# A two-block transformer kernel on one core: tokens stationary in 1024-column gemms, seven-product tiles, and low halves made by an adding DMA

## The chip, the cores and the metric

The kernel runs on one core of a Trainium2 chip. The metric is device time in microseconds, as the median of the runs; lower is better. Engines are called by their names: TensorE (PE in the profile, its weight loads PEld), VectorE (DVE), ScalarE (ACT), GpSimd (POOL) and SyncE (SP), which issues the loads.

## What is computed

Two transformer blocks over one sequence of 256 tokens, model width 2048, all in fp32. Shortened from the reference:

```python
def first_block(x, ...):
    h = rmsnorm(x, norm_attn[l])
    proj = h @ w_in[l]                       # 2048 x 6144
    ...                                      # 8 dilated heads (ya), 8 differential heads (yb)
    x = x + jnp.concatenate([ya, yb], axis=-1) @ w_out[l]
    h = rmsnorm(x, norm_ffn[l])
    x = x + (jax.nn.silu(h @ w_gate[l]) * (h @ w_up[l])) @ w_down[l]      # inner width 5632
    return rmsnorm(x, norm_final)

def second_block(x, ...):
    z = jnp.einsum('bsd,de->bse', rmsnorm_2(x, norm1_g[l]), w_in[l])
    ...                                      # 8 forgetting-attention heads, 4 mLSTM heads
    merged = (g_a * jnp.einsum('bse,ed->bsd', a_out, w_proj_a[l])
              + g_m * jnp.einsum('bse,ed->bsd', m_out, w_proj_m[l]))
    x = x + jnp.einsum('bsd,de->bse', merged, w_out[l])
    h2 = rmsnorm_2(x, norm2_g[l])
    u = causal_dwconv(jnp.einsum('bsd,df->bsf', h2, w_up[l]), conv_w[l], conv_b[l])
    ...
    return x + jnp.einsum('bsf,fd->bsd', jax.nn.silu(u_gate) * u_val, w_down[l])
```

In the text w_out, w_gate, w_up and w_down are the first block's; those of the second have a _2.

## The kernel before

Every weight is read once from HBM, and nearly all work is matrix products with them. A product of fp32 precision is made of three products of float32r operands: a number is cut into a high half (the cast to float32r) and a low half (the rest), and hi·hi, hi·lo and lo·hi are summed in PSUM. The activations are cut once and kept; the weights are cut as they arrive. `raw_tile` (L66) loads up to 2048 columns of 128 partitions into one of three buffers through SP's queue. `split` (L72) makes the halves of 1024 columns: ScalarE casts `wh` (L76), VectorE subtracts it from the raw weight and writes `wl` (L77). The pool `sp` has four slots for `wh` and four for `wl`, so these two engines run at most four halves ahead of TensorE.

There are two forms of product. In `xstat` (L102; the three attention inputs of the first block, and most of the second's) the tokens are the stationary operand and 512 weight columns move: six products of 512 columns for 128 rows of the weight and 512 of its columns, three for each half of the 256 tokens (L119 to L121). In `wstat` (L92) with `mm_w` (L80) a 128x128 block of the weight is stationary, and the tokens move: `wh` meets the 512 columns that hold the tokens' high and low halves side by side (L81), `wl` the 256 high ones (L82). Its result has features on the partitions and tokens along the row, as the residual `resid` has, so that the next stage takes it without a transpose:

```python
    def mm_w(ps, wh, wl, x, start, stop):
        pe.matmul(ps, wh, x, start=start, stop=False)
        pe.matmul(ps[:, 1, :], wl, x[:, 0, :], start=False, stop=stop)
```

`wstat` carries w_out (with a loop of its own, L384 to L404), w_gate, w_up, w_down, the mLSTM's q and k, the gates of the second block, its two projections, w_out_2, w_up_2 and w_down_2. Each result of 128 features is added to the residual as soon as it is done (L398, L399, L421, L422, L770, L771), and `hilo` cuts the new piece at once for the next stage. `Acc` (L176) gathers its squares for the norm, with an add on POOL (L188). The factor of the norm, one per token, lies along the row, and VectorE multiplies each result by it (`evac`, L408). The two feed-forward stages run in four parts of 11 chunks of the inner width: gate and up for these, then w_down over these into the residual.

PSUM is two pools of four banks, `psd` for the weight products and `psa` for all else. The order of the instructions on each engine is set when the program is built, by a scheduler that runs its own timeline; on the chip each engine keeps to it.

Of the kernel before, what the change touches and what calls it, by code (L numbers as in the profile page):

```python
# [23 lines left out]
QC = 11  # L24
NQ = FC // QC
# [5 lines left out]
GA_EARLY = 6  # L31
WARM = 8

# [19 lines left out]
def body(ctx: ExitStack, tc: tile.TileContext, xT, gp, cst, rst, w1, wo1, wg, wu, wd,  # L53
         wgate, wmo, wmv, wmq, wmk, wfox, wga, wgm, wpr, wo2, wup, wd2, out):
# [4 lines left out]
    xp = ctx.enter_context(tc.tile_pool(name="xp", bufs=16))  # L59
# [3 lines left out]
    psd = ctx.enter_context(tc.tile_pool(name="psd", bufs=4, space=PSUM))  # L63
    psa = ctx.enter_context(tc.tile_pool(name="psa", bufs=4, space=PSUM))
# [7 lines left out]
    def split(raw, a, b):  # L72
        wh = sp.tile([P, 1024], F32R, tag="wh", name="wh")
        wl = sp.tile([P, 1024], F32R, tag="wl", name="wl")
        n = b - a
        act.copy(wh[:, :n], raw[:, a:b])  # L76
        dve.tensor_sub(wl[:, :n], raw[:, a:b], wh[:, :n].bitcast(F32))  # L77
        return wh, wl

    def mm_w(ps, wh, wl, x, start, stop):  # L80
        pe.matmul(ps, wh, x, start=start, stop=False)  # L81
        pe.matmul(ps[:, 1, :], wl, x[:, 0, :], start=False, stop=stop)  # L82

    def dps():
        t = psd.tile([P, 2, S], F32, tag="d", name="d")
        return t

    def aps():
        t = psa.tile([P, 512], F32, tag="a", name="a")
        return t  # L90

    def wstat(ps, src, xs, first=True, last=True):  # L92
        raw = raw_tile(src)
        n = len(xs)
        h = (n + 1) // 2
        for a, b in ((0, h), (h, n)):
            wh, wl = split(raw, a * P, b * P)
            for k in range(a, b):
                o = (k - a) * P
                mm_w(ps, wh[:, o:o + P], wl[:, o:o + P], xs[k],  # L100
                     first and k == 0, last and k == n - 1)

    def xstat(src4, xr, pre=(), then=None):
        p0 = psd.tile([P, 512], F32, tag="d", name="d")
        p1 = psd.tile([P, 512], F32, tag="d", name="d")
        pp = (p0, p1)
        for q in range(4):
# [3 lines left out]
            for h, kn in ((0, 1), (1, 1), (2, 2)) if pre and q == 0 else ((0, 2), (2, 2)):  # L111
                wh, wl = split(raw, h * 512, (h + kn) * 512)
                for kk in range(kn):
                    k = q * 4 + h + kk
                    a, b = wh[:, kk * 512:(kk + 1) * 512], wl[:, kk * 512:(kk + 1) * 512]
                    for t in range(2):
                        xh = xr[k][:, 0, t * P:(t + 1) * P]
                        xl = xr[k][:, 1, t * P:(t + 1) * P]
                        pe.matmul(pp[t], xh, a, start=k == 0, stop=False)  # L119
                        pe.matmul(pp[t], xh, b, start=False, stop=False)  # L120
                        pe.matmul(pp[t], xl, a, start=False, stop=k == KC - 1)  # L121
        return pp

    def chunk(tag):
        t = xp.tile([P, 2, S], F32R, tag=tag, name=tag)
        return t

    def hilo(dst, src, scale=None):
        if scale is None:
            act.copy(dst[:, 0, :], src)  # L130
            dve.tensor_sub(dst[:, 1, :], src, dst[:, 0, :].bitcast(F32))
        else:
            act.activation(dst[:, 0, :], src, AF.Copy, scale=scale)
            dve.scalar_tensor_tensor(dst[:, 1, :], src, scale, dst[:, 0, :].bitcast(F32),  # L134
                                     op0=ALU.mult, op1=ALU.subtract)
# [5 lines left out]
    resid = xin[:, 16:].rearrange("p (k s) -> p k s", k=KC)  # L141
# [17 lines left out]
    def sumsq(acc):  # L159
        ps = aps()  # L160
        for t in range(2):
            pe.matmul(ps[:, t:t + 1], acc[:, t * P:(t + 1) * P], ones[:, 0:1], start=True, stop=True)
        return ps

    def bcast(r, name):
# [3 lines left out]
        ps = aps()  # L169
# [5 lines left out]
    class Acc:  # L175
        def __init__(self, name):  # L176
            self.acc = np_.tile([P, S], F32, tag=name, name=name)
            self.first = True

        def add(self, src, scale=None):  # L180
            kw = {} if scale is None else {"scale": scale}
            if self.first:
                act.activation(self.acc, src, AF.Square, **kw)
                self.first = False
            else:
                sq = np_.tile([P, S], F32, tag="sq", name="sq", bufs=2)
                act.activation(sq, src, AF.Square, **kw)  # L187
                pool.tensor_add(self.acc, self.acc, sq)  # L188

    warm = cp.tile([P, 1], F32, name="warm")  # L190
    act.copy(warm, ones[:, 0:1])
    pw = aps()
# [3 lines left out]
    first = []  # L196
    raw0 = rp.tile([P, 2048], F32, tag="raw", name="raw")
    for a, b in ((0, 1), (1, 2), (2, 4), (4, 8), (8, 12), (12, 16)):
# [4 lines left out]
        for k in range(a, b):  # L203
            c = chunk("x")
            hilo(c, resid[:, k, :], gx[:, k:k + 1])
            xr.append(c)
# [5 lines left out]
    y1 = []  # L212
    with tc.tile_pool(name="a1", bufs=1) as ap1:
# [5 lines left out]
        pool.tensor_mul(sqx, resid[:, 0:4], resid[:, 0:4])  # L219
        for i in range(1, 4):  # L220
            sqi = ap1.tile([P, 2, 4, S], F32, tag="qk", name="sqi", bufs=3)[:, 0]
            pool.tensor_mul(sqi, resid[:, 4 * i:4 * i + 4], resid[:, 4 * i:4 * i + 4])
# [4 lines left out]
        def consts():  # L227
            for d, src in ((cst_t, cst), (rst_t, rst), (gp_t, gp)):
# [22 lines left out]
        def rope_T(pp, name, hb, r2, co, so):  # L251
# [13 lines left out]
            for j in range(2):  # L265
                ps = aps()
# [24 lines left out]
        def attn_a(qT, kT, v, h):  # L291
            ps = aps()
# [16 lines left out]
            c = chunk("y")  # L309
            hilo(c, po[:, :S])  # L310
            y1.append(c)

        def attn_b(qT, kT, v, h, on, ss):
            smc, dnc = [], []
            for c in range(2):
                ps = aps()
# [27 lines left out]
            for qt in range(2):  # L344
                sq = np_.tile([P, S], F32, tag="sq", name="sq", bufs=2)
                act.activation(sq[:, :P], pv[:, qt], AF.Square, accum_out=ss[:, qt, h:h + 1])

        for grp in range(4):
# [18 lines left out]
            else:  # L367
# [7 lines left out]
                for h in range(4):  # L375
                    for t in range(2):
                        dve.tensor_scalar_mul(on[:, t, h, :], on[:, t, h, :], ss[:, t, h:h + 1])
                    ps = aps()
                    for t in range(2):
                        pe.transpose(ps[:, t * P:(t + 1) * P], on[:, t, h, :], ident)  # L380
                    c = chunk("y")
                    hilo(c, ps[:, :S], g08[:, 0:1])
                    y1.append(c)

        acc = Acc("acc")
        xr = []
        for half in range(2):
            for n2 in range(8):
                raw = raw_tile(wo1[half * 8 + n2])
                for j in range(2):  # L390
                    n = n2 * 2 + j
                    wh, wl = split(raw, j * 1024, (j + 1) * 1024)
                    ps = dps()
                    for k in range(8):
                        o = k * P
                        mm_w(ps, wh[:, o:o + P], wl[:, o:o + P], y1[8 * half + k], k == 0, k == 7)
                    t = ap1.tile([P, 2, S], F32, tag="sm", name="res", bufs=3)[:, 0]
                    dve.tensor_add(t, ps[:, 1], resid[:, n])  # L398
                    dve.tensor_add(resid[:, n], ps[:, 0], t)  # L399
                    if half == 1:  # L400
                        c = chunk("x")
                        hilo(c, resid[:, n], gain(G_FFN, n))
                        xr.append(c)
                        acc.add(resid[:, n])  # L404
        r = rtok_from(sumsq(acc.acc)[:, 0:2], "rtok", EPS)
        rb = bcast(r, "rb")

    def evac(fp, ps, rb, tag, bufs=2):  # L408
        t = fp.tile([P, S], F32, tag="ev", name="ev", bufs=3)
        act.copy(t, ps[:, 1])  # L410
        dve.tensor_add(t, ps[:, 0], t)  # L411
# [494 lines left out]
```

## Time and profile before

| | |
|---|---|
| time, median of three runs | 2571.62 us (2570.88 to 2572.28) |
| span of the profiled execution, first to last instruction | 2569.7 us |
| TensorE busy, products | 2553.7 us, 99%, 14040 |
| TensorE busy, weight loads (beside the products) | 2199.0 us, 86%, 14040 |
| VectorE busy | 1753.5 us, 68%, 2726 |
| ScalarE busy | 1317.2 us, 51%, 2069 |
| POOL busy | 72.3 us, 3%, 73 |
| read from HBM | 465.35 MB, 182 GB/s over the span |

The profiled execution has no time of its own beside its span; the runs of the table are other executions of the same program. The profile counts the time in which an engine had an instruction in work. TensorE's products overlap (one starts before the one ahead has ended), so their durations add up to more than the time they take; the pitch, from one start to the next, is what a product costs in a stream. VectorE's and ScalarE's instructions overlap a little too. A product's operands are written `d<-x,wh`: output, then moving and stationary operand in either order.

### The profile page before, as it was taken

How to read it: one execution, taken by the hardware profiler on the slowest of the kernel's cores; microseconds unless marked ns; L12 is line 12 of the kernel's file. 1: busy time of each engine (PE TensorE's matmuls, PEld its weight loads, DVE VectorE, ACT ScalarE, POOL GpSimd, SP SyncE). 2: the span in 40 equal slices, each digit the busy share in tenths (PEclk: the TensorE clock that was granted, in tenths of full speed). 3: DMA queues.
4: the chain of work that ended last, by engine and by line, in shares of the span. 5: the costliest groups of instructions: out<-in, count | busy, mean ns of one | idle time of the engine just before them, and what ended most of it. 6: DMA issues, size and time to landing. Idle time of an engine off the chain costs nothing.

```text
span 2569.7 us, 35839 instructions
## 1 busy us (share of the span) xinstructions
PE 2553.7 (99%) x14040; PEld 2199.0 (86%) x14040; DVE 1753.5 (68%) x2726; ACT 1317.2 (51%) x2069; POOL 72.3 (3%) x73
## 2 busy tenths in 40 slices
PE   8999999999999999999999999999999999999999
PEld 6888888888888888888888888888888888888888
DVE  7666578666666666677465566667777776776776
ACT  4555446444444444465455655545554554554553
POOL 3000001000000000031000000001000000000000
PEclk9999999999999999999999999999999999999999
DMA  6444445545545545545544455555555555645555
GB/s 246 152 158 170 168 164 186 191 168 209 182 172 203 186 166 205 184 165 197 186 159 164 165 182 187 197 188 182 193 184 173 208 186 171 212 171 190 198 175 168
DMA packets 73466, 469.78 MB, mean 183 GB/s; under 512 B 8144, under 2 KB 10448, under 8 KB 28496
## 3 DMA queue, kind: packets, MB, share of 16 engines
q1 hardware_dynamic: 70992, 465.38, 51.5%
q8 instruction: 110, 1.80, 0.3%
q10 hardware_dynamic: 2304, 2.10, 0.2%
q14 instruction: 60, 0.49, 0.1%
HBM read 465.35 MB, written 2.10 MB: 182 GB/s over the span
## 4 chain that ended last, share of the span: by engine, by line
PE 99%; DVE 0%; DMA 0%; issue 0%; SPq 0%; ACT 0%
PE d L81 51%; PE d L82 26%; PE d L120 6%; PE d L121 6%; PE d L119 6%; PE a L279 1%; PE a L286 0%; PE a L340 0%; PE a L270 0%; PE a L308 0%; DMA raw<-in_w 0%; DVE x L134 0%; PE d L481 0%; PE a L662 0%; PE a L671 0%
## 5 line engine op out<-in xcount | busy, mean ns | idle before, releaser
L77 DVE TENSOR_TENSOR wl<-raw,wh 128x1024 fp32r<-128x1024 f32 (+3 forms) x962 | 1095.5, 1140 | 711.1 <-ACT wh L76 702.7
L76 ACT CAST wh<-raw 128x1024 fp32r<-128x1024 f32 (+3 forms) x962 | 940.0, 979 | 1134.3 <-PE d L81 737.2
L81 PE MATMUL d<-x,wh 128*128 128x512 f32 x3456 | 1211.3, 395 | 0.0
L82 PE MATMUL d<-x,wl 128*128 128x256 f32 x3456 | 966.8, 280 | 0.0
L81 PEld LDWEIGHTS d<-x,wh 128*128 128x128 f32 x3456 | 648.1, 188 | 152.5
L81 PE MATMUL d<-y,wh 128*128 128x512 f32 x1920 | 672.3, 395 | 0.0
L82 PEld LDWEIGHTS d<-x,wl 128*128 128x128 f32 x3456 | 652.1, 189 | 0.2
L82 PE MATMUL d<-y,wl 128*128 128x256 f32 x1920 | 535.7, 280 | 0.0
L81 PEld LDWEIGHTS d<-y,wh 128*128 128x128 f32 x1920 | 359.2, 188 | 83.7
L82 PEld LDWEIGHTS d<-y,wl 128*128 128x128 f32 x1920 | 362.3, 189 | 1.2
L120 PE MATMUL d<-wl,x 128*128 128x512 f32 x704 | 278.1, 395 | 8.9 <-DVE wl L77 8.9
L119 PE MATMUL d<-wh,x 128*128 128x512 f32 x704 | 276.7, 396 | 2.2 <-ACT wh L76 2.2
L121 PE MATMUL d<-wh,x 128*128 128x512 f32 x704 | 277.0, 393 | 0.0
L120 PEld LDWEIGHTS d<-wl,x 128*128 128x128 f32 x704 | 132.8, 189 | 38.1 <-DVE wl L77 10.6
L119 PEld LDWEIGHTS d<-wh,x 128*128 128x128 f32 x704 | 132.5, 189 | 30.7 <-ACT wh L76 3.5
L121 PEld LDWEIGHTS d<-wh,x 128*128 128x128 f32 x704 | 132.8, 189 | 27.1 <-issue 0.2
L81 PE MATMUL d<-mr,wh 128*128 128x512 f32 x256 | 89.6, 393 | 0.0
L188 POOL TENSOR_TENSOR acc<-acc,sq 128x256 f32<-128x256 f32 x45 | 39.3, 874 | 1749.7 <-ACT sq L187 1749.7
L411 DVE TENSOR_TENSOR ev<-d,ev 128x256 f32<-128x256 f32 x202 | 84.2, 417 | 0.0
L410 ACT COPY ev<-d 128x256 f32<-128x256 f32 x202 | 73.4, 364 | 0.0
L82 PE MATMUL d<-mr,wl 128*128 128x256 f32 x256 | 71.3, 279 | 0.0
L421 DVE TENSOR_TENSOR res<-d,xin 128x256 f32<-128x256 f32 x128 | 53.3, 421 | 14.2 <-PE d L82 11.1
(271 smaller groups left out, 1341.2 us busy)
## 6 DMA issues: line engine op xcount, KB each, us to landing
raw<-in_wd SPq DMA_DIRECT2D x128, 704.0 KB, 4.0
raw<-in_wup SPq DMA_DIRECT2D x88, 1024.0 KB, 4.8
raw<-in_w SPq DMA_DIRECT2D x47, 1024.0 KB, 4.8
raw<-in_wg SPq DMA_DIRECT2D x44, 1024.0 KB, 4.8
raw<-in_wu SPq DMA_DIRECT2D x44, 1024.0 KB, 4.8
raw<-in_wo SPq DMA_DIRECT2D x32, 1024.0 KB, 4.7
raw<-in_wfox SPq DMA_DIRECT2D x24, 1024.0 KB, 4.8
raw<-in_wga SPq DMA_DIRECT2D x16, 1024.0 KB, 4.8
```

Of the source, the lines that this page charges most:

```text
L76: act.copy(wh[:, :n], raw[:, a:b])
L77: dve.tensor_sub(wl[:, :n], raw[:, a:b], wh[:, :n].bitcast(F32))
L81: pe.matmul(ps, wh, x, start=start, stop=False)
L82: pe.matmul(ps[:, 1, :], wl, x[:, 0, :], start=False, stop=stop)
L119: pe.matmul(pp[t], xh, a, start=k == 0, stop=False)
L120: pe.matmul(pp[t], xh, b, start=False, stop=False)
L121: pe.matmul(pp[t], xl, a, start=False, stop=k == KC - 1)
L188: pool.tensor_add(self.acc, self.acc, sq)
L279: pe.matmul(o, qT[lo:hi, a, h, qt * P:(qt + 1) * P], kT[lo:hi, b, h, :], start=i == 0, stop=i == 2)
L410: act.copy(t, ps[:, 1])
L411: dve.tensor_add(t, ps[:, 0], t)
L421: dve.tensor_add(t, ps[:, 1], resid[:, n])
```

## The change

The stages that used `wstat`, but for w_up_2 and the mLSTM's q and k, go over to one function, `gemm`. It computes 1024 output columns for all 256 tokens, with the tokens stationary and 512 weight columns moving, in four banks (two halves of the tokens, two of the columns). A tile of the weight is 256 rows (a K pair: 128 rows, then the next 128) by 1024 columns, one load of 2048 columns. On a plain tile that is 24 products.

On the first `n_sum` tiles of a gemm (2 for the gate and up weights, which are zipped into one array, and for w_down and w_down_2; 0 elsewhere) the eight block products of two by two blocks become seven. Stationary operands are blocks of the tokens or sums of them (`Pair.sums`, made once), moving ones are blocks of the weight or sums of them (`ta`, `tb`, made by VectorE for each tile, L191 to L193). Four of the products have banks of their own, three go straight into the result's, and after the second tile VectorE combines them (L216 to L220) into `plus`, which is added to the result at the end (`block`, L248, or `add_blocks`, L258 on POOL and L259 on VectorE).

On plain tiles with an odd number the low half of the second 1024 columns is not made by VectorE: ScalarE writes the negative cast into `wl` (L82), and a DMA from POOL's queue adds the raw weight to it, read a second time from HBM (L83).

Results now have tokens on the partitions. The residual is token-major too (its first value `xn` is loaded as a further constant of 2 MB), the norm's factor becomes a scale per partition, and the squares are summed by ScalarE along the row. What the next stage needs as stationary operand is turned by TensorE, four transposes of 128x128 for a pair (`turned`, L268, 216 in all), and cut in one piece of 512 columns. Inner widths of the feed-forward stages go in parts of 3, 4 and 4 groups of 512. The result is stored in four pieces of 512 KB. In the diff, cut to its core:

```diff
+    def split(src, n, again=None):
+        wh, wl = wtiles()
+        act.copy(wh[:, :n], src)
+        if again is not None:
+            act.activation(wl[:, :n], src, AF.Copy, scale=-1.0)
+            pool.dma_start(wl[:, :n], again.bitcast(F32R), accum_op=ALU.add)
+            return wh, wl
+        dve.tensor_sub(wl[:, :n], src, wh[:, :n].bitcast(F32))
+        return wh, wl
...
+        def sums(self, stag, v):
...
+            a11, a12, a21, a22 = v[:, 0, 0:P], v[:, 1, 0:P], v[:, 0, P:S], v[:, 1, P:S]
+            pool.tensor_sub(f[:, 0], a21, a22)
+            pool.tensor_sub(f[:, 2], a11, a21)
+            pool.tensor_sub(f[:, 1], f[:, 0], a11)
+            pool.tensor_add(f[:, 3], a12, f[:, 1])
...
+    def mm3(ps, ah, al, wh, wl, start, stop):
+        pe.matmul(ps, ah, wh, start=start, stop=False)
+        pe.matmul(ps, ah, wl, start=False, stop=False)
+        pe.matmul(ps, al, wh, start=False, stop=stop)
...
+    def gemm(srcs, xs, n_sum, mid=None, tag="d"):
...
+        for i in range(n_sum):
...
+            dve.tensor_add(ta, b1122, b12.unsqueeze(1).to_broadcast([P, 2, 512]))
+            dve.tensor_add(tb[:, 0], ta[:, 0], b22)
+            dve.tensor_add(tb[:, 1], tb[:, 0], b21)
...
+            wh, wl = split(b11, 512)
+            mm3(p1, *A_(0, 0), wh[:, 0:512], wl[:, 0:512], st, sp_)
+            wh, wl = split(ta.rearrange("p a b -> p (a b)"), 1024)
+            mm3(p5, *S_(0), wh[:, 0:512], wl[:, 0:512], st, sp_)
+            mm3(p7, *S_(2), wh[:, 512:1024], wl[:, 512:1024], st, sp_)
+            wh, wl = split(raw[:, 1024:2048], 1024)
+            mm3(p2, *A_(1, 0), wh[:, 0:512], wl[:, 0:512], st, False)
+            mm3(p3, *S_(3), wh[:, 512:1024], wl[:, 512:1024], st, False)
+            wh, wl = split(tb.rearrange("p a b -> p (a b)"), 1024)
+            mm3(p6, *S_(1), wh[:, 0:512], wl[:, 0:512], st, sp_)
+            mm3(p4, *A_(1, 1), wh[:, 512:1024], wl[:, 512:1024], st, False)
...
+        for i in range(n_sum, nk):
+            raw = raw_tile(srcs[i])
+            ws = [split(raw[:, j * 1024:(j + 1) * 1024], 1024,
+                        srcs[i][:, j * 1024:(j + 1) * 1024] if j == 1 and i % 2 else None) for j in range(2)]
...
+        for gi in range(ga, gb):
+            c, p = gemm(wgu[gi], xr, N_SUM, run_late)
...
+                act.activation(gt, block(c, p, t, 0), AF.Silu, scale=rt[:, t:t + 1])
...
+                dve.scalar_tensor_tensor(h, block(c, p, t, 1), rt[:, t:t + 1], gt, op0=ALU.mult, op1=ALU.mult)
...
+        for g in range(2):
+            c, p = gemm([wd[g][2 * ga + i] for i in range(n_pairs)], hs, N_SUMD, run_late)
+            add_blocks(c, p, g)
```

How instructions stand on the engines, at three places. First TensorE in the gate stage. Before, the pieces of one 1024-column half follow each other, the wide product and the narrow one by turns (`x_...` are the pieces of the activation):

```order
L81 MATMUL d_5655<-x_3175,wh_5658 128x512
L82 MATMUL d_5655<-x_3175,wl_5659 128x256
L81 MATMUL d_5655<-x_3203,wh_5658 128x512
L82 MATMUL d_5655<-x_3203,wl_5659 128x256
L81 MATMUL d_5655<-x_3235,wh_5658 128x512
L82 MATMUL d_5655<-x_3235,wl_5659 128x256
```

In the changed program the same stage's plain tile, with the second half of an odd tile at its end, `wl_5892` being written by the adding DMA:

```order
L136 MATMUL d_5667<-wh_5887,x_3392 128x512
L137 MATMUL d_5667<-wl_5888,x_3392 128x512
L138 MATMUL d_5667<-wh_5887,x_3392 128x512
L136 MATMUL d_5663<-wh_5891,x_3392 128x512
L136 MATMUL d_5664<-wh_5891,x_3392 128x512
L136 MATMUL d_5666<-wh_5891,x_3392 128x512
L137 MATMUL d_5663<-wl_5892,x_3392 128x512
L138 MATMUL d_5663<-wh_5891,x_3392 128x512
L137 MATMUL d_5664<-wl_5892,x_3392 128x512
```

All products are 512 columns wide now, and the scheduler has put three hi·hi products ahead of the first that reads the added low half.

Second, VectorE at the change from one gate and up gemm to the next (`s1`, `u3`, `u4` and `e22` of L248 are the result blocks, `h` the product of gate and up, `ta` and `tb` the weight sums, `y` the low half of a turned pair). Before, there are splits and the work on 256-column results:

```order
L77 TENSOR_TENSOR wl_5760<-raw_5757,wh_5759 128x1024
L77 TENSOR_TENSOR wl_5780<-raw_5757,wh_5779 128x1024
L411 TENSOR_TENSOR ev_5698<-d_5655,ev_5698 128x256
L413 TENSOR_TENSOR g_5701<-ev_5698,rb_3655 128x256
L77 TENSOR_TENSOR wl_5809<-raw_5806,wh_5808 128x1024
```

In the changed program, from the split that follows the old gemm's end:

```order
L85 TENSOR_TENSOR wl_6034<-raw_6009,wh_6033 128x1024
L248 TENSOR_TENSOR u3_5758<-d_5666,u3_5758 128x512
L248 TENSOR_TENSOR e22_5760<-d_5667,e22_5760 128x512
L598 SCALAR_TENSOR_TENSOR h_5992<-u4_5759,rtok_3419,gt_5989 128x512
L85 TENSOR_TENSOR wl_6044<-tb_6012,wh_6043 128x1024
L85 TENSOR_TENSOR wl_6061<-raw_6053,wh_6060 128x512
L598 SCALAR_TENSOR_TENSOR h_5998<-e22_5760,rtok_3419,gt_5995 128x512
L85 TENSOR_TENSOR wl_6068<-ta_6055,wh_6067 128x1024
L192 TENSOR_TENSOR tb_6056<-ta_6055,raw_6053 128x512
L85 TENSOR_TENSOR wl_6078<-raw_6053,wh_6077 128x1024
L193 TENSOR_TENSOR tb_6056<-tb_6056,raw_6053 128x512
L120 TENSOR_TENSOR y_6181<-a_6176,y_6181 128x512
```

The last row is followed by the split of the second tile's `tb` and those of the first plain tile. The result's blocks and the head of the next gemm now share VectorE's queue.

Third, ScalarE on an odd plain tile and the even one behind it, where it makes the casts and the negative cast:

```order
L80 CAST wh_5887<-raw_5885 128x1024
L82 ACTIVATE wl_5892<-raw_5885 128x1024
L80 CAST wh_5891<-raw_5885 128x1024
L80 CAST wh_5922<-raw_5920 128x1024
L80 CAST wh_5926<-raw_5920 128x1024
```

The negative cast stands ahead of the plain cast of the same half, so POOL's queue can issue the adding DMA first; at the first odd tile of a gemm the two stand the other way round. POOL's queue holds 97 such DMAs.

## Rows read from the trace of the kernel before

**Rows 1.** The page, part 1: busy time and share of the span by engine

```profile
PE 2553.7 (99%) x14040; PEld 2199.0 (86%) x14040; DVE 1753.5 (68%) x2726; ACT 1317.2 (51%) x2069; POOL 72.3 (3%) x73
```

**Rows 2.** The page, part 4: the chain that ended last, by engine

```profile
PE 99%; DVE 0%; DMA 0%; issue 0%; SPq 0%; ACT 0%
```

**Rows 3.** Busy time by stretch at the start: length, engines, granted clock, DMA share, GB/s

```profile
15.00:23.60 8.60, 0.27 (x2) 0.00 (x0) 8.60 (x5) 5.63 (x11) 8.44 (x5) 0.69 0.48 199
23.60:28.00 4.40, 4.37 (x10) 3.47 (x11) 4.40 (x2) 0.00 (x0) 4.32 (x2) 0.50 0.08 15
```

**Rows 4.** Stretches, L81 alone: products and weight loads, clock, DMA share, GB/s

```profile
427.00:1172.00 745.00, 737.86 (x2098) 392.99 (x2097) 1.00 0.53 187
...
1748.00:1830.00 82.00, 82.00 (x236) 43.95 (x235) 1.00 0.55 193
1830.00:2568.00 738.00, 734.95 (x2108) 394.67 (x2107) 1.00 0.54 186
```

**Rows 5.** Timeline of TensorE in an xstat stretch: start us, duration us, instruction

```profile
152.33 0.40 PE L120 MATMUL d<-wl,x 128*128 128x512 f32 x1
152.56 1.04 PE L270 MATMUL a<-cst_t,nat 128*128 128x128 f32 x8
153.36 0.48 PE L121 MATMUL d<-wh,x 128*128 128x512 f32 x1
153.67 0.40 PE L119 MATMUL d<-wh,x 128*128 128x512 f32 x1
...
159.57 0.39 PE L121 MATMUL d<-wh,x 128*128 128x512 f32 x1
```

**Rows 6.** Groups by line on TensorE: count | busy us, mean ns | idle before

```profile
L81 PE MATMUL d<-x,wh 128*128 128x512 f32 x3456 | 1211.3, 395 | 0.0
L81 PE MATMUL d<-y,wh 128*128 128x512 f32 x1920 | 672.3, 395 | 0.0
```

**Rows 7.** Timeline of VectorE, second feed-forward stage; idle time before in brackets

```profile
1902.44 1.23 DVE L77 TENSOR_TENSOR wl<-raw,wh 128x1024 fp32r<-128x1024 f32 x1 [0.18 <-ACT wh L76]
1903.59 0.42 DVE L411 TENSOR_TENSOR ev<-d,ev 128x256 f32<-128x256 f32 x1
1903.92 0.41 DVE L131 TENSOR_TENSOR y<-cv,y 128x256 fp32r<-128x256 f32 x1
```

**Rows 8.** Timeline of ScalarE, the same stage

```profile
1901.36 1.06 ACT L76 CAST wh<-raw 128x1024 fp32r<-128x1024 f32 x1 [1.22 <-PE d L81]
1902.32 0.36 ACT L410 COPY ev<-d 128x256 f32<-128x256 f32 x1
1902.58 0.41 ACT L130 CAST y<-cv 128x256 fp32r<-128x256 f32 x1
```

**Rows 9.** Groups by line and shape on ScalarE

```profile
L130 ACT CAST y<-u 128x256 fp32r<-128x256 f32 x44 | 17.7, 401 | 0.0
L133 ACT ACTIVATE x<-xin,gp_t 128x256 fp32r<-128x256 f32 x32 | 16.4, 511 | 6.7 <-DVE xin L399 6.6 <-DVE xin L771 0.2
L254 ACT ACTIVATE nat<-d,rtok 128x512 f32<-128x512 f32 x16 | 10.6, 691 | 4.2 <-PE d L121 4.0 <-DVE rtok L156 0.2
L155 ACT ACT_TABLE_LOAD x4 | 5.1, 1283 | 0.1
L271 ACT CAST kT<-a 128x512 fp32r<-128x512 f32 x8 | 4.3, 590 | 1.6 <-PE a L270 1.6
```

**Rows 10.** DMA issues by line: count, KB each, median us from issue to landing

```profile
raw<-in_wup SPq DMA_DIRECT2D x88, 1024.0 KB, 4.8
...
out<-xin ACTq DMA_DIRECT2D x16, 128.0 KB, 1.8
...
raw<-in_wpr SPq DMA_DIRECT2D x2, 512.0 KB, 3.5
```

**Rows 11.** VectorE's instructions on tile x: duration min/median/max in ns

```profile
L134 DVE SCALAR_TENSOR_TENSOR x<-xin,gp_t,x x32: 476/962/979, 382.5 to 1830.6; 128x256 fp32r<-128x256 f32 x32
```

**Rows 12.** Groups by line on POOL

```profile
L188 POOL TENSOR_TENSOR acc<-acc,sq 128x256 f32<-128x256 f32 x45 | 39.3, 874 | 1749.7 <-ACT sq L187 1749.7
```

More of the change, by code (lines that the diff above doesn't have):

```diff
@@ L111, in xstat @@
             for h, kn in ((0, 1), (1, 1), (2, 2)) if pre and q == 0 else ((0, 2), (2, 2)):
[L112 removed]
+                wh, wl = split(raw[:, h * 512:(h + kn) * 512], kn * 512)
                 for kk in range(kn):
@@ new lines, in body, with et, block, add_blocks @@
+    ET_BUFS = 10
+    def et(name):
+        t = sx.tile([P, 512], F32, tag="et", name=name, bufs=ET_BUFS)
+        return t
+    def block(c, plus, t, n):
+        if plus is None:
+            return c[t][n]
+        dve.tensor_add(plus[t][n], c[t][n], plus[t][n])
+        return plus[t][n]
+    def add_blocks(c, plus, g):
+        for t in range(2):
+            for n in range(2):
+                o = g * 1024 + n * 512
+                r = resid[:, t, o:o + 512]
+                if plus is not None:
+                    pool.tensor_add(r, r, plus[t][n])
+                dve.tensor_add(r, c[t][n], r)
@@ new lines, in turned, with pair_of @@
+    def turned(srcs, i):
+        ps = bank()
+        for j in range(2):
+            for t in range(2):
+                o = j * S + t * P
+                f = (2 * i + j) * P
+                pe.transpose(ps[:, o:o + P], srcs[t][:, f:f + P], ident)
+        return ps.rearrange("p (j s) -> p j s", j=2)
+    def pair_of(srcs, i, tag, gains=None, stag=None, pool_=xp):
+        ps = turned(srcs, i)
+        pr = Pair(tag, pool_)
+        if stag is None and gains is None:
+            pr.put2(ps)
+        elif stag is None:
+            for j in range(2):
+                pr.put(j, ps[:, j], gains[j])
+        else:
+            v = sx.tile([P, 2, S], F32, tag="sv", name="sv", bufs=2)
+            for j in range(2):
+                if gains is None:
+                    act.copy(v, ps)
+                    break
+                act.activation(v[:, j], ps[:, j], AF.Copy, scale=gains[j])
+            pr.put2(v)
+            pr.sums(stag, v)
+        return pr
@@ L173, in bcast @@
         return b
[L175 to L188, printed above, removed]
     warm = cp.tile([P, 1], F32, name="warm")
     act.copy(warm, ones[:, 0:1])
-    pw = aps()
+    pw = bank()
     for i in range(WARM):
@@ L196, in body, with run_late @@
     first = []
+    sx = None
+    late = []
+    def run_late():
+        while late:
+            late.pop(0)()
     raw0 = rp.tile([P, 2048], F32, tag="raw", name="raw")
@@ L377, in body @@
                         dve.tensor_scalar_mul(on[:, t, h, :], on[:, t, h, :], ss[:, t, h:h + 1])
-                    ps = aps()
+                    ps = bank()
                     for t in range(2):
                         pe.transpose(ps[:, t * P:(t + 1) * P], on[:, t, h, :], ident)
[L381 to L404, printed above, removed]
@@ new lines, in body @@
+    xr = xn_
+    gf = []
+    for g, n in enumerate(("ta", "tb")):
+        gf.append(sx.tile([P, 2, 512], F32, tag=n, name="gf", bufs=TT_BUFS))
+        nc.sync.dma_start(gf[g], gfr[:, 2 * g:2 * g + 2])
+    for g in range(2):
+        sq2_add(g, gf)
+    r3 = rtok_from(sq1_done(), "r3", EPS)
+    t2 = np_.tile([P, 2], F32, tag="t2", name="t2")
+    dve.tensor_mul(t2, r3, r3)
+    dve.tensor_mul(t2, sq2_done(), t2)
+    rt = rtok_from(t2, "rtok", EPS)
+    dve.tensor_mul(rt, rt, r3)
+    rb = bcast(rt, "rb")
```

530 lines of the change are left out of this document (296 added, 234 removed).

## The prediction

> **What bounds the kernel now.** I read part 1 of the page first: TensorE is busy 99% of the span, VectorE 68%, ScalarE 51% [rows 1]. Then the chain that ended last: TensorE holds 99% of it, VectorE, ScalarE and the DMAs nothing [rows 2]. Its one long wait lies at the start: from 15 to 23.6 us it is busy for 0.27 us, while VectorE is busy throughout [rows 3]. So time is TensorE's instruction count times its pitch (from one start to the next), and a change gains what it takes off that stream, less what TensorE must newly wait for. The span is 2569.7 us; the median of the runs, 2571.6, lies 1.9 above it.
>
> **The pitch of the two forms.** A 128x128 weight block meets 256 tokens either as one 512-column and one 256-column product (L81, L82) or, with the tokens stationary, as 1.5 products of 512 columns. The first form: the stage from 427 to 1172 us runs 2112 pairs by the program (88 x 16 of w_gate and w_up, 44 x 16 of w_down; the row shows 2098 of them) in 745 us, 0.353 a pair; the stage from 1830 to 2568 the same number in 738, 0.349; w_out_2 236 in 82, 0.3475 [rows 4]. The second: 26 products start between 153.67 and 159.57 us, 0.2269 each [rows 5]. The pair's pitch differs by 1.6% between stages; as much on 0.2269 would be 0.0036, which I keep as a bound.
>
> **Removed and added on TensorE.**
> - Before: 5632 pairs, those of [rows 6] and the 256 of w_out_2: 745 + 738 + 1408 x 0.3475 (489) = 1972 us; with 2112 products of xstat x 0.2269 (479) 2451.
> - After, by counting the order: 8118 products of 512 columns x 0.2269 = 1842, and 1536 pairs that stay (w_up_2, the mLSTM's q and k) x 0.349 = 536. Together 2378. The gain is 73 us: 138 products fewer by the seven-product tiles (46 tiles x 3) are 31 of it, the shape the rest. The slower pitch would take 8118 x 0.0036 = 29 back: 44 to 73.
> - Added: 216 transposes. Eight of them push the stream from 152.33 to 153.67, 1.34 us, of which two products are 0.45 [rows 5]: 0.111 each, 24 us.
>
> **Added: the head of a seven-product gemm.** Here VectorE can become late. On a plain tile TensorE works 24 x 0.2269 = 5.4 us and VectorE 1.15 or 2.3; on a seven-product tile TensorE works 21 x 0.2269 = 4.8 and VectorE makes the sums and splits 3584 columns. Its pitch is 1.15 for 1024 columns and 0.33 for 256 [rows 7], so about 0.6 for 512; ScalarE's cast has 0.96 [rows 8]. With four wh/wl slots, two splits of the first tile are ready when the last product of the gemm before ends (T). VectorE then does, in the order shown, from about T-0.3: raw split 1.15, two blocks 1.2, h 0.65, tb split 1.15, 512 split 0.6, h 0.65, ta split 1.15, tb 0.6, raw split 1.15, tb 0.6, y 0.6, to T+9.2; the last cast (tb is complete at T+8.6, 0.1 to see it, 0.96) ends at T+9.7 and the last tb split at T+10.9. The cast of the tile behind ends at T+10.65. TensorE's own work to that point is 42 products (9.5), eight transposes (0.9) and four products of the tile behind that need no wl (0.9), 11.3 in all; but three of these four follow at 10.65 to 11.3, the four held products to 12.2, the last to 12.45. So it waits 1.15 us in each of 11 w_gate/w_up gemms, 13 us. In the 12 w_down gemms VectorE's list lacks two h and a y (-1.9) and TensorE's the transposes (-0.9): 0.15 each, 2. Sum 15; bounds 0, and 43 if each instruction takes its full duration (1.23 [rows 7], 0.69) in place of its pitch (2.3 and 1.5 us a gemm).
>
> **Added: the adding DMA.** 97 low halves go this way. The slot frees when TensorE ends its half; until the same slot is read again TensorE has 39 products (8.8 us), 36 (8.2) at the first odd tile. ScalarE's negative cast is not in the trace: it lies between the plain cast (1.05) and, by the ratio of a scaled to a plain 256-column copy (511 to 401 [rows 9]), 1.35; I take 1.15, nearer the plain one. That leaves 7.6 us for POOL's issue and the flight, 6.1 at the 23 first odd tiles, where the plain cast goes first. The nearest flight is the 512 KB load, 3.5 us [rows 10]; the far end is that behind a 1 MB load in flight, 3.5 + 4.8 = 8.3. I take cost zero, because the load of that size is the nearest row and the DMA engines are half idle (share 0.53 to 0.55 [rows 4]); zero is also the lower bound. The upper: 23 x 2.2 + 74 x 0.7 = 103 us. The Trainium skill, DMA: Bandwidth & Descriptors, section "Anatomy of one DMA — SWDGE (gpsimd) path", fits a transfer from GpSimd as 2.0 us plus its bytes over 436 GB/s; by that an estimate is 3.2 us, hidden too, and no run here has shown such a transfer.
>
> **Added: boundaries.** Before, the residual came out 128 columns at a time and x with it. Now the last blocks end together. After w_out the four banks that the transposes need hold its result. ScalarE's list ahead of the second tile's first cast is 12 scalings (0.51 long, 0.41 in pitch by rows 8: 4.9), three squares (2.1), four 512-column casts (2.4), a table load (1.3) and that cast (0.5), 11.2 us [rows 9]; TensorE has 32 transposes (3.6) and 21 products (4.8) for it, so it waits 2.8. Four scalings and three casts of the second tile follow, 4.5 us, beside which TensorE has almost nothing: 7 us in all. The other two such places have half of x ready and begin with it: 1 us each. Sum 9, bounds 0 and 20. Behind the long wait at the start the granted clock stood at 0.50 for 4.4 us, the lower level of 1.2 GHz [rows 3]. That would add some 2 us at one boundary; the bound holds it. **The end:** the last store is 512 KB, whose load lands in 3.5 us, instead of 128 KB (1.8) [rows 10]: +2.
>
> POOL's 48 residual adds, 56 small sums and 8 gate adds I cost at nothing: the order puts the adds beside plain tiles, where VectorE has 3 us of each 5.4 free.
>
> **Sum:** -73 + 24 + 15 + 0 + 9 + 2 = -23. On the span 2546.7 us; beside the median 2548.6.
>
> **The rivals.**
> 1. *The adding DMA is late (slower).* Place: TensorE's products with wl on odd tiles. For it: the trace has no such transfer, its destination must be read too, and it runs beside a 1 MB load every 5.4 us. Against: 7.6 us of room. It decides from a flight of 6.1 us on. At 8.3: 2548.6 + 103 = 2652.
> 2. *VectorE sets the heads.* With full durations the heads cost 43, not 15: 2577, the edge of no change. For it: ScalarE and VectorE take turns through one slot. Against: rows 7 show pitch, not duration, wherever work is ready.
> 3. *POOL and VectorE hold each other up.* VectorE's two-tensor scaling takes 476 ns at best but 962 at the median, where POOL's adds of 874 run beside it [rows 11, 12]: 486 a time. POOL gains 56 adds of 512 columns (twice the row's 256: 1.75 us) and 56 of 128 (0.44), 122 us; at 486 per 874 that is 68 us of VectorE. If it all fell into heads: 2617. The Trainium skill, SBUF — State Buffer, section "Who interferes with whom", has it as a rule that a VectorE instruction with two SBUF inputs and a GpSimd one that reads SBUF contend for one port; rows 11 agree. Against the price: the order keeps nearly all of it beside plain tiles.
> 4. *Nothing waits.* Heads and boundaries are hidden: 2548.6 - 24 = 2525. For it: the heads are 5 us beside plain tiles of 33 in which VectorE idles. Against: the head's list is longer than TensorE's.
>
> **How the numbers follow.** A measurement cannot tell less than about 0.2%, 5.1 us, from no change, so 2566.5 to 2576.8 counts as the same. My case (2530 to 2572) has 0.52, of it 0.05 above 2566.5. Nothing waits: 0.15. Late DMA: 0.16. VectorE heads: 0.11 (0.02 faster, 0.06 same, 0.03 slower). POOL: 0.06 (0.02 faster, 0.04 slower). Faster 0.47 + 0.15 + 0.02 + 0.02 = 0.66; same 0.05 + 0.06 = 0.11; slower 0.16 + 0.03 + 0.04 = 0.23. The range, 2515 to 2620, takes in rivals 2, 3 and 4, the slower pitch (2548.6 + 29 = 2578) and the milder half of a late DMA; the rest of that is left out above, and a little below.
>
> **What would show it.** Right: some 8118 products of 512 columns at 0.227; transposes at 0.11; 0 to 2 us of waiting for VectorE's wl at each seven-product gemm; one gap of 5 to 10 us after w_out; adding DMAs that land in under 6 us. Wrong: TensorE's waits on the DMA of wl over 20 us in all, or on VectorE over 40; 1024-column splits well above 1.23 us; a pitch off 0.227 by more than 0.003.

## The result, and the profile after

The changed kernel takes 2757.66 us (median of 4 runs, 2755.5 to 2769.0) against 2571.49 us before: a ratio of 1.073, 95% interval 1.0718 to 1.0743. Forecast was 2548.6 with a range of 2515 to 2620. The profiled execution is the longest of the four (span 2767.2). The page of the changed kernel, parts 1 and 4:

```profile
PE 2607.1 (94%) x12050; PEld 2121.6 (77%) x12050; DVE 1708.2 (62%) x2257; ACT 1433.7 (52%) x1979; POOL 242.4 (9%) x222
...
PE 23%; DMA 4%; ACT 1%; issue 0%; DVE 0%; DVEq 0%; ACTq 0%
```

TensorE has 1990 instructions fewer than in [rows 1] and is busy 94% of a longer span; DMAs hold 4% of the chain that ended last, where [rows 2] had 0%. What TensorE waits for (us in all, times, longest):

```profile
PE d L137 <- DMA wl<-in_wgu: 54.6, 30, 4.8
PE d L137 <- DMA wl<-in_wd: 50.2, 25, 4.1
PE d L137 <- DVE wl L85: 12.2, 4, 7.8
PE d L137 <- DMA wl<-in_wgs: 7.1, 11, 1.0
...
PE a L137 <- DMA wl<-in_wo: 1.7, 4, 0.5
...
PE d L137 <- DMA wl<-in_wo: 1.5, 4, 0.6
```

The adding DMAs are late 74 times, 115.1 us in all. (Of the wait for VectorE's `wl`, 11.2 us lie in the first 60 us, where the kernel before waits too.) The DMA issues of the changed kernel say why, in their last column, the median time from issue to landing, called the flight here:

```profile
raw<-in_wgu SPq DMA_DIRECT2D x88, 1024.0 KB, 6.3
...
wl<-in_wgu POOLq DMA_DIRECT2D x33, 512.0 KB, 8.2
wl<-in_wd POOLq DMA_DIRECT2D x32, 512.0 KB, 8.7
...
wl<-in_wo POOLq DMA_DIRECT2D x16, 512.0 KB, 8.0
```

An adding DMA of 512 KB takes longer than a load of 1 MB, and 2.3 times the 3.5 us of the 512 KB load in [rows 10]. The timeline of a gate gemm, first odd tile and the next (start, duration, instruction, idle before); the SPq row merges loads, of which two have started when the adding DMA goes out, at 551.99 and 553.76:

```profile
551.99 6.83 SPq L70 DMA_DIRECT2D raw<-in_wgu  x3
...
551.66 1.05 ACT L80 CAST wh<-raw 128x1024 fp32r<-128x1024 f32 x1
552.61 1.06 ACT L82 ACTIVATE wl<-raw 128x1024 fp32r<-128x1024 f32 x1
...
553.96 0.86 POOL L83 DMA_DIRECT2D wl<-in_wgu  x1 [24.82 <-DVE wl L85]
...
558.67 1.07 PE L136 MATMUL d<-wh,x 128*128 128x512 f32 x4
563.29 0.79 PE L137 MATMUL d<-wl,x 128*128 128x512 f32 x1 [3.55 <-DMA wl<-in_wgu]
563.88 0.63 PE L138 MATMUL d<-wh,x 128*128 128x512 f32 x1
564.30 0.63 PE L137 MATMUL d<-wl,x 128*128 128x512 f32 x1
...
566.59 1.06 ACT L82 ACTIVATE wl<-raw 128x1024 fp32r<-128x1024 f32 x1 [6.67 <-PE d L137]
...
567.94 0.86 POOL L83 DMA_DIRECT2D wl<-in_wgu  x1 [13.12 <-ACT wl L82]
...
576.05 0.50 PE L137 MATMUL d<-wl,x 128*128 128x512 f32 x1 [0.39 <-DMA wl<-in_wgu]
576.39 0.39 PE L138 MATMUL d<-wh,x 128*128 128x512 f32 x1
```

At the first odd tile ScalarE works without a pause, and the negative cast comes up at 552.61, behind the plain cast of the same half (551.66). The DMA goes out at 553.96 and is read at 563.29, 9.3 us later; TensorE has done its four products that need no `wl` and waits 3.55 us. (The row names VectorE's `wl` as what POOL waited for; that split ended at about the same time as the negative cast, and at both places the DMA starts 0.29 us behind the cast.) Behind the wait TensorE's pitch is 0.42 to 0.43 (563.88, 564.30), nearly twice that of [rows 5]. At the next odd tile the cast starts when TensorE frees the slot (566.59), the DMA goes out at 567.94 and is read 8.1 us later, 0.39 late.

Two things differ between the places. One is the room, the time from the DMA's start to where TensorE would have read without waiting: 9.33 - 3.55 = 5.8 us at the first odd tile, 8.11 - 0.39 = 7.7 at the next. Over all 23 first odd tiles its mean is 6.0. The other is the flight. At most places a 1 MB load starts within 1 us behind the adding DMA, and those ahead have landed or nearly so; there the median is 8.1 us. At the first odd tiles loads are already on their way, and it is 9.5. At the last two adding DMAs of the program, when no load is left, it is 5.4:

```profile
DMA to landing us min/median/max: 5.4/5.4/5.4
```

The granted clock of the stretches around the long wait (length, TensorE busy, clock, DMA share, GB/s):

```profile
552.00:559.00 7.00, 7.00 (x33) 1.00 0.87 268
559.00:566.00 7.00, 3.45 (x10) 0.78 0.81 257
566.00:576.00 10.00, 9.66 (x42) 0.98 0.64 164
```

So a long wait is paid twice: as idle time, and at the lower level (1.2 GHz) behind it.

### The profile page after: what moved, and what is told of

Its sections match the earlier page's. It is cut to its first block, busy times and chain, and to the rows that moved or that the text cites. A ratio compares the mean times of both kernels' runs of the same rounds, so it can differ in the third digit from the quotient of the medians.

```text
span 2767.2 us, 31441 instructions
## 1 busy us (share of the span) xinstructions
PE 2607.1 (94%) x12050; PEld 2121.6 (77%) x12050; DVE 1708.2 (62%) x2257; ACT 1433.7 (52%) x1979; POOL 242.4 (9%) x222
## 3 DMA queue, kind: packets, MB, share of 16 engines
q0 software_dynamic: 13968, 50.86, 11.2%
## 5 line engine op out<-in xcount | busy, mean ns | idle before, releaser
L85 DVE TENSOR_TENSOR wl<-raw,wh 128x1024 fp32r<-128x1024 f32 (+1 forms) x785 | 967.0, 1236 | 826.6 <-ACT wh L80 823.9
L80 ACT CAST wh<-raw 128x1024 fp32r<-128x1024 f32 (+1 forms) x882 | 899.6, 1025 | 843.6 <-PE d L138 517.0
L137 PE MATMUL d<-wl,x 128*128 128x512 f32 x1532 | 619.4, 404 | 74.6 <-DMA wl<-in_wgu 54.6
L138 PE MATMUL d<-wh,x 128*128 128x512 f32 x1532 | 611.6, 400 | 0.7 <-DMA raw<-in_wgu 0.7
L136 PE MATMUL d<-wh,x 128*128 128x512 f32 x1532 | 569.8, 397 | 5.4 <-ACT wh L80 3.7
L141 PE MATMUL a<-x,wh 128*128 128x512 f32 x1536 | 544.8, 400 | 0.0
L142 PE MATMUL a<-x,wl 128*128 128x256 f32 x1536 | 432.7, 282 | 0.0
L136 PEld LDWEIGHTS d<-wh,x 128*128 128x128 f32 x1532 | 290.0, 190 | 71.9 <-ACT wh L80 9.8
L141 PEld LDWEIGHTS a<-x,wh 128*128 128x128 f32 x1536 | 289.9, 189 | 71.8
L138 PEld LDWEIGHTS d<-wh,x 128*128 128x128 f32 x1532 | 295.7, 193 | 61.0 <-DVE x L120 1.2
L142 PEld LDWEIGHTS a<-x,wl 128*128 128x128 f32 x1536 | 291.7, 190 | 0.2
L138 PE MATMUL d<-wh,y 128*128 128x512 f32 x624 | 252.7, 405 | 0.0
L82 ACT ACTIVATE wl<-raw 128x1024 fp32r<-128x1024 f32 x97 | 102.8, 1060 | 237.1 <-PE d L137 224.8
L136 PE MATMUL d<-wh,y 128*128 128x512 f32 x624 | 217.2, 397 | 1.7 <-ACT wh L80 1.7
```

The costliest lines, as they stand in the source:

```text
L80: act.copy(wh[:, :n], src)
L82: act.activation(wl[:, :n], src, AF.Copy, scale=-1.0)
L85: dve.tensor_sub(wl[:, :n], src, wh[:, :n].bitcast(F32))
L136: pe.matmul(ps, ah, wh, start=start, stop=False)
L137: pe.matmul(ps, ah, wl, start=False, stop=False)
L138: pe.matmul(ps, al, wh, start=False, stop=stop)
```

## The experiments

The first question was whether the late DMA is the whole loss. **noadd** takes the adding DMAs out:

```diff
-                        srcs[i][:, j * 1024:(j + 1) * 1024] if j == 1 and i % 2 else None) for j in range(2)]
+            ws = [split(raw[:, j * 1024:(j + 1) * 1024], 1024) for j in range(2)]
```

> The changed kernel without the adding DMAs: VectorE makes all low halves. Theory A (the adding DMA is late; its waits of 115 us, the refill of TensorE's stream behind them and the lower clock after them are all that the prediction missed): 2549 us, between 2535 and 2565. Theory B (heads and boundaries cost more than forecast, hidden behind the DMA waits, and VectorE gets 97 splits of 1.22 us more): 2600 to 2680.

2578.9 us (10 runs, 2576.1 to 2582.72; 1.0025 of before, interval 1.0016 to 1.0034). So the adding DMAs cost 178.8 us, net of the 97 splits that VectorE makes in their place, and the time is still 30 us above the forecast: neither theory gave this number. The four gate gemms of part 2, first of the changed kernel:

```profile
668.42:880.90 212.48, 187.01 (x769) 0.95 0.62 188
```

then of noadd:

```profile
632.19:808.25 176.06, 173.94 (x769) 1.00 0.55 191
```

The same 769 instructions take 36.4 us more with 12 adding DMAs, 3.0 us a DMA; in the stages of w_gs and the second block's projections, which have no heads, 16 DMAs cost 9.2 us, 0.6 each (229.56 against 220.37 us).

**noadd_nosum** sets `N_SUM = N_SUMD = 0` besides:

> Neither adding DMAs nor seven-product tiles: every tile has 24 products. If the heads of seven-product gemms cost the 15 us forecast, this is 31 - 15 = 16 us slower than the kernel without adding DMAs alone, some 2565 us; if the heads are hidden, 31 us slower; if they cost 43, 12 us faster.

2577.3 us (interval of the ratio 1.0013 to 1.0033, nearly that of noadd). None of the three outcomes named came: the 138 products that the seven-product tiles save are worth nothing. Where the saving goes is seen by stages: gate and up of part 1 and of part 2, then w_down of part 2 and of part 3. noadd:

```profile
428.80:567.06 138.26, 133.44 (x584) 0.99 0.50 177
...
808.25:895.21 86.96, 86.45 (x381) 1.00 0.56 194
...
1071.21:1164.70 93.49, 89.71 (x400) 0.98 0.56 194
```

The kernel without seven-product tiles:

```profile
426.80:561.25 134.45, 134.45 (x609) 1.00 0.54 184
...
627.50:804.50 177.00, 177.00 (x793) 1.00 0.55 190
804.50:892.51 88.01, 88.01 (x393) 1.00 0.55 193
...
1069.51:1159.53 90.02, 90.02 (x411) 1.00 0.52 184
```

In part 2 (for noadd the 176.06 us above) four gate gemms save 24 products, 5.4 us, and keep 0.9: a head, the first two tiles of such a gemm with their sums and splits, costs 1.1. Two w_down gemms save 2.7 and keep 1.05: 0.8 a head. Part 1 and the last w_down become longer, by 3.8 and 3.5 us.

**scratch** has noadd's VectorE work, and beside it casts and adding DMAs into a tile of its own (`wm`), which nobody reads:

```diff
+            wm = wmx.tile([P, 1024], F32R, tag="wm", name="wm", bufs=1)
+            act.activation(wm[:, :n], src, AF.Copy, scale=-1.0)
+            pool.dma_start(wm[:, :n], again.bitcast(F32R), accum_op=ALU.add)
```

> VectorE makes all low halves, and at the 65 places of w_gate/w_up, w_down and w_down_2 ScalarE's negative cast and the adding DMA still run, into a tile that nobody reads (the 32 of w_gs, w_out and w_out_2 are left out). Theory A (only the waiting for the data costs): within 5 us of the kernel without adding DMAs. Theory C (the second read, the traffic into SBUF or ScalarE's extra work disturbs the loads and the splits): 10 to 60 us more than that.

2592.5 us, 13.6 more than noadd: theory C, at its lower end. The loads of `raw` for the feed-forward weights land in 5.6 us instead of 4.8 and 4.9, and TensorE's waits for ScalarE's `wh` go from 5.8 to 11.6 us. The adding DMAs themselves land sooner here, in 7.5 us (gate and up) and 5.9 (w_down) at the median. Where the loads ahead have landed or nearly so and the next starts 1 us or more behind, the median is 5.5: the flight depends on the loads beside it too.

**plainwrite** drops `accum_op=ALU.add`:

> The same DMA from the same queue writes the raw weight into the low half instead of adding it (the low halves so made are the raw weight, not its low part). If the adding makes the flight long (the destination has to be read, and the sum formed), it lands in 3.5 to 5 us instead of 8.3 and the time is about 2560 us; if the queue and the descriptors make it long, it still lands in about 8 us and the time stays near 2757.

One run, 2649.4 us. Its queue totals (packets, MB, share of the 16 engines) and DMA issues:

```profile
q0 software_dynamic: 13968, 50.86, 7.5%
...
wl<-in_wgu POOLq DMA_DIRECT2D x33, 512.0 KB, 4.9
```

its waits:

```profile
PE d L137 <- DMA wl<-in_wgu: 21.5, 11, 3.2
PE d L137 <- DMA wl<-in_wd: 20.0, 10, 3.1
```

and the same queue of the changed kernel:

```profile
q0 software_dynamic: 13968, 50.86, 11.2%
```

The adding lengthens the flight: 4.9 us without, 8.2 with, for the same bytes and packets, which take 7.5% of the engines in place of 11.2%. At the last two of these DMAs, with no load on its way, it is 4.1 against 5.4:

```profile
DMA to landing us min/median/max: 4.1/4.1/4.1
```

The time was a miss: TensorE still waits 41.5 us, at 20 of the 23 first odd tiles and at one other tile. The median hides these places. One of them, its DMA and its reader:

```profile
542.46 0.53 POOL L83 DMA_DIRECT2D wl<-in_wgu  x1 [24.45 <-DVE wl L85]
...
549.70 0.50 PE L137 MATMUL d<-wl,x 128*128 128x512 f32 x1 [1.49 <-DMA wl<-in_wgu]
```

The flight is 7.2 us there, and the room 7.24 - 1.49 = 5.75, as in the changed kernel. At all 20 the flight is 5.6 to 9.5 us, behind loads that are already on their way; there even a plain write was late.

**half** sends only the second 512 columns that way:

```diff
-            act.activation(wl[:, :n], src, AF.Copy, scale=-1.0)
-            pool.dma_start(wl[:, :n], again.bitcast(F32R), accum_op=ALU.add)
+            act.activation(wl[:, 512:n], src[:, 512:n], AF.Copy, scale=-1.0)
+            pool.dma_start(wl[:, 512:n], again[:, 512:n].bitcast(F32R), accum_op=ALU.add)
+            dve.tensor_sub(wl[:, :512], src[:, :512], wh[:, :512].bitcast(F32))
```

> The adding DMA and the negative cast carry only the second 512 columns of the half (256 KB); VectorE makes the low half of the first 512. If the flight goes with the bytes, it lands in 4 to 6 us, the waits fall to some 30 us and the time to about 2620; if it is mostly fixed, it lands in 7 to 8 us and the time stays above 2700.

One run, 2581.9 us. Its waits for the DMA, and its DMA issues:

```profile
PE d L138 <- DMA wl<-in_wd: 0.8, 2, 0.6
...
PE d L138 <- DMA wl<-in_wgu: 0.2, 1, 0.2
```

```profile
wl<-in_wgu POOLq DMA_DIRECT2D x33, 256.0 KB, 4.5
wl<-in_wd POOLq DMA_DIRECT2D x32, 256.0 KB, 5.5
```

With half the bytes the flight is 4.5 and 5.5 us, the waits are gone (1.0 us), and the time is noadd's. That is better than expected (2620). It is not the flight alone: up to 9.1 us is seen at first odd tiles here too. But the negative cast is half as long, and the added half is read some products later; where TensorE waits in the first block, the room is 8.5 us, against 5.7 to 6.1 at most first odd tiles of plainwrite.

**slots2** gives the low half that the DMA adds into two slots of its own:

```diff
+        if again is not None:
+            wl = wmx.tile([P, 1024], F32R, tag="wm", name="wm", bufs=2)
```

> The 65 adding DMAs of w_gate/w_up, w_down and w_down_2 get two slots of their own for the low half (the 32 of w_gs, w_out and w_out_2 are left out, there is no room), so the negative cast and the DMA can go out some 2.7 us earlier on a plain tile and more at a first odd tile. Theory A (the flight of 8.2 us stays, only the room is short): TensorE waits under 15 us in all for these DMAs, and the time is 2575 to 2600 us. Theory D (more room only lets the flights grow, or ScalarE's queue holds the cast back as before): waits above 60 us, time above 2650.

2604.4 us (4 runs, 2598.69 to 2609.89). The flights stay long (7.4 and 7.3 us), the waits nearly go:

```profile
PE d L141 <- DMA wm<-in_wd: 7.6, 5, 2.5
...
PE d L141 <- DMA wm<-in_wgu: 1.4, 1, 1.4
```

Theory A: the room was short. The time lies 4 us above its bound, and 25 above noadd: 9 of it are these waits, and most of the rest would be the traffic and the negative casts, if they cost what they did in scratch (13.6).

**notfirst** leaves the 23 first odd tiles behind seven-product tiles to VectorE (`if j == 1 and i % 2 and (i > 3 or n_sum == 0)`):

> The 23 first odd tiles of the gemms with seven-product tiles are made by VectorE; 74 adding DMAs stay. Theory A (two classes: some 3.6 us at each first odd tile, where ScalarE's queue is full, and about 0.5 us at the others; only the long ones lower the clock): waits on the DMAs of 30 to 40 us, hardly any time at the lower clock in the feed-forward stages, about 2625 us. Theory E (whatever tile comes first waits long): waits above 80 us and 2680 us or more.

One run, 2672.2 us, between the two: 51.1 us of waits for the DMAs, the longest 3.4. Part of the lateness moves to the odd tile behind, where the room is 7.4 to 7.9 us and the flight up to 10.8.

**add_nosum** keeps the adding DMAs and has no heads (`N_SUM = N_SUMD = 0`):

> Adding DMAs as in the changed kernel, but no seven-product tiles: every gemm starts with plain tiles, and there are 120 adding DMAs instead of 97. Theory A (the long waits of some 3.6 us come from ScalarE's queue at the head of a seven-product gemm, which holds the negative cast back; elsewhere a tile is some 0.5 us late): no wait above 2 us, 50 to 60 us of waits in all, little time at the lower clock behind them, about 2645 us. Theory E (any first odd tile of a gemm waits long): 27 waits above 3 us, over 120 us in all, about 2750 us.

One run, 2664.2 us; the clock over the span is 0.997 (0.977 in the changed kernel):

```profile
PE d L137 <- DMA wl<-in_wd: 23.0, 37, 2.4
PE d L137 <- DMA wl<-in_wgu: 21.3, 35, 1.7
...
PE d L137 <- DMA wl<-in_wgs: 8.0, 11, 1.6
...
PE d L137 <- DMA wl<-in_wo: 2.3, 7, 0.7
```

Theory A in its numbers: 94 waits, 56 us, two above 2 us, and no time to speak of at the lower clock. 120 such DMAs cost 87 us without heads; 97 cost 179 with them. Without a head the first odd tile of most gate gemms has a room of 7.9 us, not 6.0, and a flight of 8.0, not 9.5. That ScalarE's queue is what makes the difference, as theory A says, is not shown: the head also brings loads closer together. The time is 19 above the forecast; of the 87, 6 are not accounted for by waits (56) and refills (25, below).

Next, the other 30 us. **latebcast** makes the norm's row for w_up_2 behind the first result:

> Without adding DMAs, and the norm factor's row for the second feed-forward stage is made behind the first result of w_up_2 instead of ahead of it. The kernel without adding DMAs waits 7.0 us there for VectorE and runs 6.8 us at the lower clock behind it. If that boundary is what the forecast missed there: 2569 us, 10 less than the kernel without adding DMAs; if the wait only turns up at w_up_2's operands instead: no change, 2579.

2577.3 us (9 runs, 2573.56 to 2580.5; interval of the ratio 1.0012 to 1.0032, which overlaps noadd's): no difference clear of noise. The 7.0 us for `dg` (L357), a part of the norm's row, are gone, and 4.3 us for VectorE's pieces `x` (L115) have come at the same place. So the row's place in the order was not the cause; VectorE's work on the residual ends too late either way.

**downsum** (`N_SUM = 0`, `N_SUMD = 2`), and **early**, which adds to it:

```diff
+            if g == 1:
+                pre = []
+                for n in (0, FC):
+                    pre.append(bank())
+                    wstat(pre[-1], wup[n][:, 0:1024], xr, last=False)
```

> No adding DMAs, and seven-product tiles in w_down and w_down_2 alone (24 tiles). By the stages of the kernel without adding DMAs against the one that has no seven-product tiles either, those of w_gate/w_up cost as much as they save and those of w_down save 1.1 to 1.3 us a part: 2570 us, 7 less than without any. If the heads of w_down take back what the products save too: 2577.

> As the one before, and TensorE gets work for the boundary before w_up_2: the first halves of its first two results (16 pairs, 5.6 us) stand ahead of the transposes of the last four pairs of the residual. If the wait of 7.0 us there and the lower clock behind it are idle time that such work covers: 8 to 10 us less than the kernel before it, about 2561 us. If VectorE's and ScalarE's chain just ends later: no difference.

downsum 2574.4 us (2570.5 to 2577.31), between the two outcomes named: the last w_down of the first block is longer there too, 94.24 us. early 2565.6 (0.9976 of before, 0.9966 to 0.9985), 8.8 less, as forecast: the boundary was idle time that other work can fill. **early2** takes the seven-product tiles from that last w_down gemm:

```diff
-            c, p = gemm([wd[g][2 * ga + i] for i in range(n_pairs)], hs, N_SUMD, run_late)
+            c, p = gemm([wd[g][2 * ga + i] for i in range(n_pairs)], hs, N_SUMD if part < 2 or g == 0 else 0, run_late)
```

> As the kernel with work for the boundary, and the last w_down gemm of the first block has no seven-product tiles, so its first products do not need banks that the transposes of the residual still hold. There TensorE waits 3.2 us and runs 6.8 us at the lower clock; in the kernel without seven-product tiles the same stretch is 4.2 us shorter. If the banks are the cause: 4 to 5 us less than the kernel before it, about 2561 us. If VectorE's pieces of the residual are late for their own sake: 1.4 us more, 2567.

2560.82 us (5 runs, 2560.54 to 2561.36), 0.9958 of before, 0.9944 to 0.9971: 0.4% faster than the kernel before. It is 4.7 less than early, as forecast if the banks are the cause. In downsum TensorE has one long wait there:

```profile
PE a L136 <- DVE x L115: 3.2, 1, 3.2
```

The product that waits does not read `x`; its operand is `y`, the pieces of the product of gate and up. So what it needs is the bank, which VectorE frees when it has read the residual's transposes. In early2 this wait is gone; besides the start, where the kernel before waits too, its largest sum of waits is

```profile
PE d L136 <- ACT wh L80: 2.0, 3, 1.0
```

## Why the prediction was wrong

**The adding DMA at zero: the step that failed.** The prediction took the flight from the 512 KB load (3.5 us) "because the load of that size is the nearest row". A load does not add, and the load of [rows 10] says nothing of the loads beside it. The steps from 3.5 us to what was measured are: 4.1 for a plain write from POOL's queue with no load on its way, 5.4 with the adding, 8.1 beside a 1 MB load that starts just behind, 9.5 at the first odd tiles. The rooms were right: 7.6 us were put for the issue and the flight, 6.1 at the first odd tiles, and 7.7 and 6.0 are measured from the DMA's start, which is 0.3 us behind the cast's end. So the term that failed is the flight, and not the room.

The rival of a late DMA had 0.16, and both its reasons (the destination must be read too, loads run beside it) fit the runs. That its 8.3 us are so near the median is partly luck: they were the sum of two loads, one waiting for the other, and at most places no load is ahead of the DMA. Its price, 23 x 2.2 + 74 x 0.7 = 103, is near the 115.1 us of waits, though split otherwise: the waits at the 23 first odd tiles, added from the timeline, are 82.6 us, 3.6 each, and the other 51 are 32.5. Two things the rival left out:
- The refill. The product ahead of a wait takes its 0.39 us instead of a pitch of 0.227, and the one behind the wait has a pitch of 0.34 (576.05 to 576.39): 74 x 0.27 = 20 us.
- The lower clock. A mean granted clock of 0.977 over 2767.2 us with levels 1 and 0.5 means 127 us at the lower; noadd's 0.994 over 2578.6 means 31. The 96 between cost at most half, 48 us.

115 + 20 + 48 = 183, at most, of the 189 us between the two profiled executions. The page agrees: against noadd TensorE is idle for 116 us more (160.1 against 44.1) and busy for 73 more (2607.1 against 2534.5), and the refill and the lower clock are busy time.

The Trainium skill, DMA: Bandwidth & Descriptors, section "Anatomy of one DMA — SWDGE (gpsimd) path", has a fit by which 3.2 us was the estimate; the trace does not agree: the plain write of plainwrite took 4.1 with no load beside it and 4.9 at the median. The Trainium skill, Collectives: The Full Stack, section "Stop ④ — SDMA + CCE: where bytes move and the add happens", counts an adding transfer as two reads and a write, "with the add free in between". No run here parts the add from the second read; together they took 11.2% of the engines against 7.5% for the same packets.

**The product stream: right.** The prediction's terms give 3168 x 0.2269 + 88 x 0.111 = 729 us for the first feed-forward stage without seven-product tiles; noadd_nosum takes 732.7 (426.80 to 1159.53), against 745 in [rows 4].

**Heads: right in kind, too small.** 1.15 us a gate gemm was forecast, 1.1 measured in part 2; 0.15 a w_down gemm, 0.8 measured. The first gemm behind w_out and the last w_down came on top: there the sums, and banks that the transposes still hold, come late. The forecast is 2548.6 with heads and 2548.6 + 31 - 15 = 2564.6 without; measured, without adding DMAs, are 2578.9 and 2577.3. So the heads and their places cost 31 + 1.6 = 33 us, not 15, and the forecast lacks a further 12.7 that have nothing to do with heads.

**Boundaries: the wrong one.** 7 us were put behind w_out and 1 each at the others. noadd_nosum waits 1.3 behind w_out and 7.0 before w_up_2, with the lower clock behind it (0.85 over the 16 us that follow): its timeline and windows there

```profile
1833.28 1.19 PE L359 MATMUL a<-dg,ones 128*128 128x256 f32 x2 [6.97 <-DVE dg L357]
```

```profile
1834.00:1850.00 16.00, 16.00 (x81) 0.85 0.18 67
```

"Half of x is ready" was true but did not help: the norm's row stood ahead of it in TensorE's order, and with the row moved behind (latebcast) the other half of `x` came late instead. early, which puts 5.6 us of other work there, took 8.8 us off.

**The rivals.** POOL and VectorE do hold each other up, as the third rival said, but TensorE does not feel it. Behind the first 60 us, the 66 of VectorE's 1024-column splits that overlap work on POOL take 1.71 us on average, the other 747 take 1.22; yet TensorE's waits for `wl` from VectorE there are 1.0 us in all. That bears out the reason given against it, that this work lies beside plain tiles. "Nothing waits" (2525) is refuted, with and without the DMA. The second rival's 2577 is near the 2578.9 without adding DMAs by luck: its heads cost 43 us, the measured ones 33, and the 12.7 us lie elsewhere.

Together: 2548.6 + 12.7 (neither heads nor adding DMA; the boundary before w_up_2 gave back 8.8) + 17.6 (heads) + 178.8 (adding DMA) = 2757.7. The parts are differences between the runs, so that they add up is no test of its own.

## What to carry to other kernels

A transfer of a kind that the trace does not show is not priced by the nearest size: here the adding and the loads beside it made 8 us and more of the 3.5 that were forecast. Ask which loads are in flight when it starts, even where the DMA engines are half idle on average. Where its buffer is freed by its own reader, a flight longer than the room is late nearly every time; two more slots (slots2) or fewer bytes read later (half) took the waits away. Price a wait of TensorE with what follows it, the refill and, behind a long one, the lower clock. Fewer products gained nothing where each group of them needed a head on other engines: give that head cover, or leave it out where it has none (early2).

## What was not expected of the hardware

- Adding costs a DMA of 512 KB from POOL's queue 3.3 us beside the loads (medians of 8.2 and 4.9), but 1.3 when no load is on its way (5.4 and 4.1). Half the bytes take about half the time beside the loads (4.5), but alone 4.2 against 5.4.
- 94 waits of up to 2.4 us left the mean clock at 0.997; behind waits of 3.55 and 6.97 us TensorE ran at nearly twice its pitch for some 3 and 5 us.
- A DMA into a tile that nobody reads, with its negative cast, still cost 0.2 us each (13.6 us for 65), beside later loads and longer waits for casts.
